# Holding small TensorE steps for a partner, and a placing model with measured durations, in a hybrid S5 and DeltaNet layer

## The chip, the cores and the metric

The kernel runs on one core of a Trainium2 chip. The metric is the device time of one execution in microseconds. Before the change it is 2961.34 us, the median of three runs (2958.78 to 2963.57).

## What is computed

One residual layer on x of 1024 frames by 2048 channels, in float32:

```python
h = rmsnorm(x, ln_w)
proj = h @ w_in                     # 2048 x 10256: u, z_s, q, k, v, z_d, beta, a, gate_s, gate_d
y_s = s5_mixer(u, z_s, ...) @ w_up_s        # 64 groups, 64 complex states each, scan over time, GELU, GLU
y_d = deltanet_mixer(q, k, v, z_d, ...) @ w_up_d   # 8 heads x 128, short conv, chunked delta rule
mixed = sigmoid(gate_s) * y_s + sigmoid(gate_d) * y_d
out = rmsnorm(x + mixed @ w_out, final_norm_w)
```

The delta rule needs, for each head and chunk, the inverse of a unit lower triangular matrix, and then a recurrence over the chunks; S5 needs small projections into and out of its states and a scan over time.

## The kernel before

**Passes and blocks.** The sequence is cut in two passes of T = 512 frames. A pass is a written-out list of blocks. First come ba, then for each head h the blocks k, q, v, z, gd, gd and, shifted by a head or two, u (S5's input). Then come zs (8 blocks, with the last u between them), ud (16), gs (16), glu (8), us (16) and the output projection in four groups of 512 columns. Each block is a product of 128 output channels by 512 frames over 16 k tiles of 128 (8 in ud, glu and us). A k tile takes three f32r matmuls of 128x128 by 512: weights and activations are split in a high and a low part, and hi*hi, hi*lo and lo*hi are added. These are the large products. Weights arrive by DMA in `raw`; `w_prep` copies the high part on ScalarE (`whi`) and subtracts it on VectorE (`wlo`), one chunk of four k tiles at a time. `w_next` keeps LA = 4 chunks split ahead. In the profile's rows X, Y, G0a and G0b are blocks of SBUF that hold the split activations or S5's and the setup's data, and M is the block with DeltaNet's data.

**Lanes.** All other work is written as Python generators, one for each task, queued in lanes: epi (evictions of a block), io (single DMAs), chain (the recurrence of a head, `d_chain`), prep (a head's decay, products and inverse, `d_prep`), tab (S5's tables), s5 (S5's setup `s5_setup`, then `s5_gen` for each of 8 groups of channels), out, and x (`x_gen`, which loads, scales and transposes the next pass's input during the output projection). After each k tile (in the output projection, after each three matmuls) `pump()` goes once over the lanes, and `step(lane)` resumes the first generator of a lane up to its next yield. What the step issues lands at that place in the instruction stream of each engine. The engines run their streams in order, so a step on TensorE that comes before its operands are there holds up every large product behind it.

**The placing model.** While the program is built, `Timed` wraps each engine and books a duration for each instruction in `Clock`, with the data it waits for. A lane's step is taken if its operands are ready on the model's TensorE clock (`job[2] > clk["PE"]` returns) and if the model's VectorE clock is not ahead of TensorE's by more than the lane's slack: 1 us for s5 and tab, 3 for prep, out and x, 4 for chain, SETUP = 2 for the setup. `yield -1` makes the next step ready at once. A head's prep or chain is late when the block number `now` passes its head by more than LATE = 1.0 or 1.4; its slack is then 8, and s5 and tab stand still.

**Drains.** At some places a lane is emptied at once whatever the clocks say (`drain`): epi and io after each block, prep and chain of head i-2 before head i goes on, everything of DeltaNet before ud, s5 before glu, x at the end of the output projection. `d_chain` drains the setup before it writes its first output (`drain("s5", -1)` after its four last transposes), since the setup's scratch lies in that block.

**A head's small products.** `d_prep` has ten steps on TensorE: transposes of k (T), two steps pA (128x128 by 256), transposes of v, then six steps of the inverse, four in 32x32 pieces and two in 64x64. Between pA and the inverse stand 30 small products on GpSimd and a round trip through DRAM (`lu_d`, `tu_d`). `d_chain` has 13 steps on TensorE: three for each of four chunks and a last one with transposes; it starts from `chain_after`, which polls with a bare `yield` until the head's prep is through. `until` polls with `yield -1` until q or v of the head is there. S5 has two steps for each of two halves of a group: the projection into the states (64x128 by 256) and out of them (mostly 128x64 by 256).

Of the kernel before, what the change touches and what calls it, by code (L numbers as in the profile page):

```python
# [18 lines left out]
WAIT = 0.2  # L19
SETUP = 2.0  # L20
LATE = (1.0, 1.4)
MAGIC = float(1.5 * 2 ** 23)
MAGICB = float(1.5 * 2 ** 23 + 127)
LOG2E = float(np.float32(math.log2(math.e)))
# [19 lines left out]
class Clock:  # L44
# [6 lines left out]
    def __init__(self):  # L51
        self.t = {"PE": 0.0, "V": 0.0, "S": 0.0, "G": 0.0, "Q": 0.0, "D": 0.0}
        self.wr, self.rd, self.last = {}, {}, 0.0
        self.slot = {}
        self.table = None

    def cells(self, a):
        name = a.tensor.name
        name = self.slot.get(name) or name.rsplit("_", 2)[0]
        if a.space == bass.MemoryType.DRAM:  # L60
            n = 1 + sum((c - 1) * abs(st) for st, c in a.ap)
            lo, hi = a.offset // 65536, (a.offset + n - 1) // 65536
            return [(name, i) for i in range(lo, hi + 1)]
        ps = a.ap[0][0]
        q = a.offset // ps
        lo = a.offset % ps
        hi = lo + sum((c - 1) * abs(st) for st, c in a.ap[1:])
        parts = range(q // 32, (q + a.ap[0][1] - 1) // 32 + 1)
        return [(name, h, i) for h in parts for i in range(lo // self.CELL, hi // self.CELL + 1)]
# [24 lines left out]
class Timed:  # L94
    def __init__(self, eng, key, clock):
        self.eng, self.key, self.clock = eng, key, clock

    def __getattr__(self, name):
        f = getattr(self.eng, name)
        if name not in COST:  # L100
            return f

        def g(*a, **k):
            o = a[0]
            ck = self.clock
            n = o.free_size()
            ins = [v for v in a[1:] if isinstance(v, bass.AP)]
            ins += [v for kk, v in k.items() if isinstance(v, bass.AP) and kk != "accum_out"]
            outs = [o]
            if self.key == "PE":  # L110
                if name == "transpose":
                    c = 0.11
                elif k["rhs"].dtype == F32R:
                    c = n / 2400
                else:
                    rows = k["lhsT"].shape[0]
                    c = max(n / 600, 0.06) * (0.3 if o.shape[0] <= 32 else 0.5 if min(o.shape[0], rows) <= 64 else 1.0)
                lat = 0.1
            elif name == "dma_start":
                c, lat = 4.0 * n * o.shape[0], 0  # L120
            else:
                fix, per = COST[name][self.key]
                c, lat = fix + per * n, 0.16
                if k.get("op") == ALU.pow:
                    c = 0.25 + 0.17 * n
                if name == "activation":
                    if "accum_out" in k:
                        c += 0.09
                        outs.append(k["accum_out"])
                    fn = a[2] if len(a) > 2 else k["func"]  # L130
                    if fn in TABLES and TABLES[fn] != ck.table:
                        ck.table = TABLES[fn]
                        c += 1.28
            ck.run(self.key, c, outs, ins, lat, name == "dma_start")
            return f(*a, **k)  # L135
        return g


TABLES = {AF.Tanh: 0, AF.Exp: 0, AF.Sin: 1, AF.Ln: 2}
_VG = {"V": (0.07, 1.04e-3), "G": (0.14, 2.1e-3), "S": (0.05, 0.9e-3)}  # L140
_VF = {"V": (0.1, 0.6e-3), "G": (0.12, 1.1e-3), "S": (0.05, 0.9e-3)}
COST = {"tensor_tensor": _VG, "scalar_tensor_tensor": _VG, "tensor_scalar": _VF, "tensor_copy": _VF,
        "tensor_reduce": _VG, "activation": _VG, "tensor_tensor_scan": {"V": (0.07, 1.28e-3)},
        "memset": _VF, "reciprocal": {"V": (0.07, 8.3e-3)}, "iota": _VG, "matmul": None, "transpose": {"V": (0.07, 1.04e-3)}, "dma_start": None}


@with_exitstack
def kernel(
# [25 lines left out]
    clock = Clock()  # L174
    clk = clock.t
    V = Timed(nc.vector, "V", clock)
    S = Timed(nc.scalar, "S", clock)
    G = Timed(nc.gpsimd, "G", clock)
    PE = Timed(nc.tensor, "PE", clock)
# [33 lines left out]
    def tt(o, a, b, op, eng=None):  # L213
        (eng or V).tensor_tensor(o, a, b, op=op)

    def ts(o, a, s1, s2, op0, op1=None):
        if op1 is None:
            V.tensor_scalar(o, a, s1, None, op0=op0)
        else:
            V.tensor_scalar(o, a, s1, s2, op0=op0, op1=op1)  # L220

    def stt(o, a, s, b, op0, op1):
        V.scalar_tensor_tensor(o, a, s, b, op0=op0, op1=op1)
# [76 lines left out]
    def exp_parts(xin, n, scr):  # L300

        c, k, r, q, s = (scr[:, i * n:(i + 1) * n] for i in range(5))
        ts(c, xin, -170.0, 127.0, MAX, MIN)
        ts(k, c, LOG2E, MAGIC, MUL, ADD)
        ts(k, k, MAGIC, None, SUB)
        stt(r, k, -LN2_HI, c, MUL, ADD)
        stt(r, k, -LN2_LO, r, MUL, ADD)
        ts(q, r, 1.0 / 5040, None, MUL)
        for d in (720, 120, 24, 6, 2, 1):
            stt(q, q, 1.0 / d, r, ADD, MUL)  # L310
        ts(c, k, 0.5, MAGIC, MUL, ADD)
        ts(c, c, MAGIC, None, SUB)
        tt(k, k, c, SUB)
# [134 lines left out]
    lanes = {"epi": [], "io": [], "chain": [], "prep": [], "tab": [], "s5": [], "out": [], "x": []}  # L448
    slack = {"epi": 99.0, "io": 99.0, "chain": 4.0, "prep": 3.0, "s5": 1.0, "tab": 1.0, "out": 3.0, "x": 3.0}
# [3 lines left out]
    def late(lane, h):  # L453
        return h >= 0 and now[0] > h + {"prep": LATE[0], "chain": LATE[1]}[lane]

    def late_any():
        return any(lanes[n] and late(n, lanes[n][0][0]) for n in ("prep", "chain"))

    def step(lane):
        q = lanes[lane]  # L460
        while q:
            job = q[0]
            lag = slack[lane] if job[0] >= 0 else SETUP
            if lane in ("chain", "prep") and late(lane, job[0]):
                lag = 8.0
            elif lane in ("s5", "tab") and job[0] >= 0 and late_any():
                return
            if job[2] > clk["PE"] or clk["V"] - clk["PE"] > lag:
                return
            clock.last = 0.0  # L470
            try:
                wait = next(job[1]) or 0.0
            except StopIteration:
                q.pop(0)
                continue
            job[2] = 0.0 if wait < 0 else max(clock.last, wait) + WAIT
            return

    def pump():
        for lane in lanes:  # L480
            step(lane)

    def add(lane, key, gen, at=None):
        lanes[lane].append([key, gen, max(clk["V"], clk["S"]) if at is None else at])
# [117 lines left out]
    def s5_setup(ga, gb, yb):  # L602
# [31 lines left out]
        def vv():  # L634
            a = yb[:, k0[0]:k0[0] + N]
            k0[0] += N
            return a
# [9 lines left out]
        kk, r, hh, ah, s1, c1 = vv(), vv(), vv(), vv(), vv(), vv()  # L647
        ts(kk, th_, INV2PI, MAGIC, MUL, ADD)
        ts(kk, kk, MAGIC, None, SUB)
        stt(r, kk, -PI_C1, th_, MUL, ADD)  # L650
# [735 lines left out]
    for ps_ in range(NPASS):  # L1386
# [49 lines left out]
        for kind, i, c0 in plan[ps_]:  # L1436
# [74 lines left out]
            for k4 in range(nkt // 4):  # L1511
                hi, lo = w_next()
                if kind == "ba":
                    h3 = hi.rearrange("p (k c) -> p k c", k=4)
                    for kl in range(4):
                        kt = k4 * 4 + kl
                        mh, ml = mov(kind, kt)
                        PE.matmul(pb[0:32, :], lhsT=h3[:, kl, 0:32], rhs=mh, start=(kt == 0), stop=False)
                        PE.matmul(pb[0:32, :], lhsT=h3[:, kl, 0:32], rhs=ml, start=False, stop=(kt == nkt - 1))
                        pump()  # L1520
                    continue
                for kl in range(4):
                    kt = k4 * 4 + kl
                    mh, ml = mov(kind, kt)
                    wh, wl = hi[:, kl * P:(kl + 1) * P], lo[:, kl * P:(kl + 1) * P]
                    PE.matmul(pb, lhsT=wh, rhs=mh, start=(kt == 0), stop=False)
                    PE.matmul(pb, lhsT=wh, rhs=ml, start=False, stop=False)
                    PE.matmul(pb, lhsT=wl, rhs=mh, start=False, stop=(kt == nkt - 1))
                    pump()
# [87 lines left out]
        for g in range(4):  # L1617
            pbs = [bank((mainb[0] % 2, 3, 4, 1 - mainb[0] % 2)[t]) for t in range(4)]

            def mm(kt, t, hi, lo):  # L1620
                a, b = (z[:, t * P:(t + 1) * P] for z in kt_of(mh_, kt))
                PE.matmul(pbs[t], lhsT=a, rhs=hi, start=(kt == 0), stop=False)
                PE.matmul(pbs[t], lhsT=a, rhs=lo, start=False, stop=False)
                PE.matmul(pbs[t], lhsT=b, rhs=hi, start=False, stop=(kt == KT - 1))
                pump()
# [68 lines left out]
```

## Time and profile before

| | |
|---|---|
| median of three runs | 2961.34 us |
| profiled execution: time, span | 2961.29 us, 2959.6 us |
| TensorE matmul busy | 2908.3 us, 98% |
| VectorE, ScalarE, GpSimd busy | 1681.5, 1151.8, 410.2 us |
| granted TensorE clock | 0.996 |
| moved by DMA | 409.52 MB, 138 GB/s |

The profile names engines PE (TensorE), PEld (its weight loads), DVE (VectorE), ACT (ScalarE), POOL (GpSimd) and SP. A row of a group gives line, engine, operation, the tile written and the tiles read, then a count, busy time, mean ns of one, and the idle time of the engine ahead of it with what ended that. All instructions go through the wrapper, so all have line 135. A row of the timeline gives start and duration; its x is the count of like instructions that it merges. Matmuls overlap: one of 512 columns shows as 0.39 us long while the next starts after 0.226. A stage's row gives its bounds and length, the busy time and count of PE, PEld, DVE, ACT and POOL, the granted clock, the DMA share and GB/s.

### The profile page before, as it was taken

Reading aid. Unit: us, or ns where it says so; the run is one execution under the profiler, and the core shown is the slowest. Engines: PE = TensorE matmul, PEld = TensorE weight load, DVE = VectorE, ACT = ScalarE, POOL = GpSimd, SP = SyncE. Lnnn points to the kernel's source line nnn. Section 1 sums busy time; section 2 is a strip of 40 time slices with the busy share of each in tenths; the row PEclk is TensorE's granted clock in tenths of the full one; section 3 lists DMA queues with packets and bytes.
Section 4 is the critical chain, followed back from the end, with each engine's and each line's share of the span. In section 5 each row is a group of like instructions: output and inputs, shape, how many; then the busy total and the mean of one; then the engine's idle time right before and its main releaser. Section 6 shows DMA issues by size and latency. Waiting matters only on the chain.

```text
span 2959.6 us, 42410 instructions
## 1 busy us (share of the span) xinstructions
PE 2908.3 (98%) x15840; PEld 2335.3 (79%) x15840; DVE 1681.5 (57%) x3194; ACT 1151.8 (39%) x2487; POOL 410.2 (14%) x792
## 2 busy tenths in 40 slices
PE   8998999999999999999999999999999999999998
PEld 6876777777777788888877777777777788888887
DVE  5746777776767722563444775667656632236542
ACT  5434555554454322334333344333433322223331
POOL 4420222122200000000024211222022000000000
PEclk9999999999999999999999999999999999999999
DMA  6525455445445554446355444544444654445641
GB/s 172 131 74 149 122 132 143 121 123 148 120 128 172 169 149 117 148 136 231 132 164 138 121 122 126 143 124 127 122 139 119 177 171 121 124 123 152 207 138 57
DMA packets 620641, 409.52 MB, mean 138 GB/s; under 512 B 91546, under 2 KB 551571, under 8 KB 618515
## 3 DMA queue, kind: packets, MB, share of 16 engines
q1 hardware_dynamic: 618130, 398.42, 47.1%
q0 software_dynamic: 2304, 8.39, 0.8%
q8 instruction: 125, 2.05, 0.3%
q14 instruction: 82, 0.66, 0.1%
HBM read 339.98 MB, written 66.75 MB: 137 GB/s over the span
## 4 chain that ended last, share of the span: by engine, by line
PE 85%; DVE 5%; POOL 4%; DMA 3%; issue 2%; ACT 2%; SPq 1%; DVEq 0%; POOLq 0%; ACTq 0%
PE p L135 85%; POOL M L135 3%; DVE M L135 1%; DVE G0a L135 1%; DVE wlo L135 1%; DVE Y L135 1%; DMA M<-tu_d 1%; SPq L135 1%; DMA lu_d<-M 1%; ACT M L135 1%; POOL ex L135 1%; DVE tmp L135 0%; DMA M<-lu_d 0%; ACT whi L135 0%; DMA tu_d<-M 0%
## 5 line engine op out<-in xcount | busy, mean ns | idle before, releaser
L135 PE MATMUL p<-X,whi 128*128 128x512 f32 (+1 forms) x4432 | 1395.4, 397 | 2.4 <-DVE whi L135 0.8
L135 DVE TENSOR_TENSOR wlo<-raw,whi 128x512 fp32r<-128x512 f32 x920 | 630.9, 700 | 685.0 <-ACT whi L135 684.0
L135 PEld LDWEIGHTS p<-X,whi 128*128 128x128 f32 (+1 forms) x4432 | 804.7, 187 | 177.3 <-issue 17.5
L135 PE MATMUL p<-X,wlo 128*128 128x512 f32 (+1 forms) x2184 | 852.8, 390 | 10.9 <-DVE wlo L135 10.8
L135 ACT ACTIVATE whi<-raw 128x512 fp32r<-128x512 f32 x917 | 556.0, 625 | 512.2 <-PE p L135 452.9
L135 PE MATMUL p<-Y,whi 128*128 128x512 f32 (+1 forms) x1808 | 568.8, 396 | 0.9 <-ACT p L135 0.9
L135 PEld LDWEIGHTS p<-X,wlo 128*128 128x128 f32 x2184 | 411.0, 188 | 99.9 <-DVE wlo L135 12.0
L135 PEld LDWEIGHTS p<-Y,whi 128*128 128x128 f32 (+1 forms) x1808 | 330.3, 187 | 72.8 <-issue 5.6
L135 PE MATMUL p<-Y,wlo 128*128 128x512 f32 x896 | 349.9, 391 | 2.1 <-DVE wlo L135 2.1
L135 ACT ACTIVATE tmp<-p 128x512 f32<-128x512 f32 x160 | 95.6, 598 | 404.6 <-PE p L135 381.9
L135 POOL TENSOR_TENSOR M<-M 32x28 f32<-32x28 f32 (+8 forms) x492 | 198.9, 404 | 273.7 <-DMA M<-lu_d 185.9
L135 POOL TENSOR_SCALAR smalls<-smalls 128x4 f32<-128x4 f32 (+1 forms) x58 | 15.1, 261 | 1574.7 <-DVE smalls L135 1076.1
L135 DVE TENSOR_TENSOR G0a<-G0a 128x256 f32<-128x256 f32 (+1 forms) x432 | 210.6, 524 | 7.5 <-ACT G0a L135 4.2
L135 PEld LDWEIGHTS p<-Y,wlo 128*128 128x128 f32 x896 | 168.1, 188 | 38.9 <-DVE wlo L135 3.0
L135 PEld LDWEIGHTS p<-M 32*32 32x32 f32 (+2 forms) x3072 | 123.1, 122 | 74.9 <-ACT M L135 27.9
L135 PE MATMUL p<-M 32*32 32x32 f32 (+3 forms) x3072 | 157.2, 216 | 9.0 <-DMA M<-tu_d 3.9
L135 ACT ACTIVATE M<-p 32x128 f32<-32x128 f32 (+3 forms) x323 | 89.9, 281 | 113.8 <-PE p L135 110.4
L135 DVE SCALAR_TENSOR_TENSOR tmp<-tmp,vec 128x512 f32<-128x512 f32 x144 | 108.0, 750 | 9.2 <-ACT tmp L135 5.8
L135 DVE TENSOR_TENSOR G0a<-p,G0a 128x512 f32<-128x512 f32 x128 | 82.0, 682 | 29.2 <-PE p L135 29.2
L135 DVE TENSOR_TENSOR_SCAN G0a<-rho,scar,G0a 128x256 f32<-128x256 f32 x128 | 89.1, 736 | 0.0
L135 PE MATMUL p<-whi,G0a 128*128 128x512 f32 x280 | 88.5, 391 | 0.0
L135 ACT ACTIVATE M<-M 128x128 f32<-128x128 f32 (+2 forms) x98 | 40.2, 412 | 119.5 <-DVE M L135 106.7
(207 smaller groups left out, 2624.6 us busy)
## 6 DMA issues: line engine op xcount, KB each, us to landing
raw<-in_w_in_dram SPq DMA_DIRECT2D x324, 512.0 KB, 4.0
raw<-in_w_out_dram SPq DMA_DIRECT2D x56, 512.0 KB, 4.1
raw<-in_dn_w_up_dram SPq DMA_DIRECT2D x32, 512.0 KB, 4.0
raw<-in_s_w_up_dram SPq DMA_DIRECT2D x32, 512.0 KB, 3.8
td_d<-tmp SPq DMA_DIRECT2D x32, 256.0 KB, 2.3
M<-tu_d SPq DMA_DIRECT2D x32, 256.0 KB, 3.2
cs_d<-G0a SPq DMA_DIRECT2D x32, 256.0 KB, 3.7
yg_d<-G0a SPq DMA_DIRECT2D x64, 128.0 KB, 3.0
```

The source lines that it names most:

```text
L135: return f(*a, **k)
```

## The change

Two things. The placing model gets other durations, and a step that begins on TensorE is held for a while.

Durations (us; n is the number of elements in a partition):

```diff
                 elif k["rhs"].dtype == F32R:
-                    c = n / 2400
+                    c = n / 2400 + 0.0137
+                    if self.apart:
+                        c += 0.09
+                        self.apart = False
                 else:
-                    rows = k["lhsT"].shape[0]
-                    c = max(n / 600, 0.06) * (0.3 if o.shape[0] <= 32 else 0.5 if min(o.shape[0], rows) <= 64 else 1.0)
+                    part = min(o.shape[0], k["lhsT"].shape[0])
+                    c = 0.05 if part <= 32 else max(n / 960, 0.15) if part <= 64 else max(n / 600, 0.2)
+                    if part <= 64 and not self.apart:
+                        c += 0.1
+                    self.apart = True
...
-                        c += 0.09
+                        c += 0.19
...
-_VG = {"V": (0.07, 1.04e-3), "G": (0.14, 2.1e-3), "S": (0.05, 0.9e-3)}
-_VF = {"V": (0.1, 0.6e-3), "G": (0.12, 1.1e-3), "S": (0.05, 0.9e-3)}
+_VG = {"V": (0.17, 1.04e-3), "G": (0.33, 1.95e-3), "S": (0.2, 0.82e-3)}
+_VF = {"V": (0.17, 0.6e-3), "G": (0.22, 1.3e-3), "S": (0.2, 0.82e-3)}
```

`apart` is set by any small f32 product and cleared by the next large one. The pairs are a fixed part and a part for each element. The scan goes from (0.07, 1.28e-3) to (0.1, 2.5e-3), VectorE's transpose from 0.07 to 0.17 fixed. A small f32 matmul of the program shows as two instructions in the profile (a transpose as one).

Holding:

```diff
+HOLD = 6
...
+    on_pe, turns = {}, [0]
+
+    def place(gen):
+        while gen.gi_yieldfrom is not None:
+            gen = gen.gi_yieldfrom
+        return gen.gi_code, gen.gi_frame.f_lineno if gen.gi_frame else 0
...
     def step(lane):
...
+            at = place(job[1])
+            clock.last, clock.products = 0.0, 0
...
+            on_pe[at] = on_pe.get(at, False) or clock.products > 0
...
     def pump():
+        wait = []
         for lane in lanes:
-            step(lane)
+            job = ready(lane)
+            if job is not None:
+                if on_pe.get(place(job[1])):
+                    wait.append(lane)
+                else:
+                    step(lane)
+        if wait:
+            turns[0] += 1
+            if len(wait) > 1 or turns[0] >= HOLD or late_any():
+                turns[0] = 0
+                for lane in wait:
+                    step(lane)
```

`ready` holds the conditions that `step` had. `place` is the line at which a generator stands, and `on_pe` remembers the places from which a resume has issued a TensorE product at least once. A lane at such a place waits until a second lane does so too, until six pumps have counted, or while a head's prep or chain is late. Everything the step issues is held with it, products, evictions and DMAs. `drain` is as before.

More of the change, by code (lines that the diff above doesn't have):

```diff
@@ L55, in __init__ @@
         self.table = None
+        self.products = 0
     def cells(self, a):
@@ L110, in g @@
             if self.key == "PE":
+                ck.products += 1
                 if name == "transpose":
@@ L113, in g @@
                 elif k["rhs"].dtype == F32R:
-                    c = n / 2400
-                else:
-                    rows = k["lhsT"].shape[0]
-                    c = max(n / 600, 0.06) * (0.3 if o.shape[0] <= 32 else 0.5 if min(o.shape[0], rows) <= 64 else 1.0)
+                    c = n / 2400 + 0.0137
+                    if self.apart:
+                        c += 0.09
+                        self.apart = False
+                else:
+                    part = min(o.shape[0], k["lhsT"].shape[0])
[3 more added lines that the diff above has]
+                    self.apart = True
                 lat = 0.1
@@ L139 @@
 TABLES = {AF.Tanh: 0, AF.Exp: 0, AF.Sin: 1, AF.Ln: 2}
-_VG = {"V": (0.07, 1.04e-3), "G": (0.14, 2.1e-3), "S": (0.05, 0.9e-3)}
-_VF = {"V": (0.1, 0.6e-3), "G": (0.12, 1.1e-3), "S": (0.05, 0.9e-3)}
+_VG = {"V": (0.17, 1.04e-3), "G": (0.33, 1.95e-3), "S": (0.2, 0.82e-3)}
+_VF = {"V": (0.17, 0.6e-3), "G": (0.22, 1.3e-3), "S": (0.2, 0.82e-3)}
 COST = {"tensor_tensor": _VG, "scalar_tensor_tensor": _VG, "tensor_scalar": _VF, "tensor_copy": _VF,
-        "tensor_reduce": _VG, "activation": _VG, "tensor_tensor_scan": {"V": (0.07, 1.28e-3)},
-        "memset": _VF, "reciprocal": {"V": (0.07, 8.3e-3)}, "iota": _VG, "matmul": None, "transpose": {"V": (0.07, 1.04e-3)}, "dma_start": None}
+        "tensor_reduce": _VG, "activation": _VG, "tensor_tensor_scan": {"V": (0.1, 2.5e-3)},
+        "memset": _VF, "reciprocal": {"V": (0.07, 8.3e-3)}, "iota": _VG, "matmul": None, "transpose": {"V": (0.17, 1.04e-3)}, "dma_start": None}
 @with_exitstack
@@ L457, in late_any, with ready @@
         return any(lanes[n] and late(n, lanes[n][0][0]) for n in ("prep", "chain"))
-    def step(lane):
[L460 to L466, printed above, removed]
+    def ready(lane):
+        q = lanes[lane]
+        if not q:
+            return None
+        job = q[0]
+        lag = slack[lane] if job[0] >= 0 else SETUP
+        if lane in ("chain", "prep") and late(lane, job[0]):
+            lag = 8.0
+        elif lane in ("s5", "tab") and job[0] >= 0 and late_any():
+            return None
+        if job[2] > clk["PE"] or clk["V"] - clk["PE"] > lag:
+            return None
+        return job
+    on_pe, turns = {}, [0]
[3 more added lines that the diff above has]
+        return gen.gi_code, gen.gi_frame.f_lineno if gen.gi_frame else 0
+    def step(lane):
+        while True:
+            job = ready(lane)
+            if job is None:
                 return
-            if job[2] > clk["PE"] or clk["V"] - clk["PE"] > lag:
-                return
-            clock.last = 0.0
+            at = place(job[1])
+            clock.last, clock.products = 0.0, 0
             try:
@@ L473, in step @@
             except StopIteration:
-                q.pop(0)
+                lanes[lane].pop(0)
                 continue
+            on_pe[at] = on_pe.get(at, False) or clock.products > 0
             job[2] = 0.0 if wait < 0 else max(clock.last, wait) + WAIT
@@ L479, in pump @@
     def pump():
+        wait = []
         for lane in lanes:
-            step(lane)
+            job = ready(lane)
+            if job is not None:
[9 more added lines that the diff above has]
+                    step(lane)
     def add(lane, key, gen, at=None):
```

## The prediction

> **What bounds the kernel now.** I read the head of the page, then busy time by stage, then the list of who waited for whom on TensorE in the two stages that hold small products, then single stretches of the timeline.
>
> ```profile
> span 2959.6 us, 42410 instructions
> PE 2908.3 (98%) x15840; PEld 2335.3 (79%) x15840; DVE 1681.5 (57%) x3194; ACT 1151.8 (39%) x2487; POOL 410.2 (14%) x792
> PE 85%; DVE 5%; POOL 4%; DMA 3%; issue 2%; ACT 2%; SPq 1%; DVEq 0%; POOLq 0%; ACTq 0%
> ```
>
> TensorE is the bound, and 85% of the chain that ended last is its own work. The table by stage (length, then busy time and instructions of each engine) shows where anything is left:
>
> ```profile
> 218.00:230.00 12.00, 1.38 (x6) 0.88 (x5) 11.69 (x12) 1.11 (x2) 0.00 (x0) 0.72 0.07 25
> 230.00:933.00 703.00, 694.54 (x4263) 549.38 (x4263) 507.17 (x1054) 359.97 (x788) 120.98 (x260) 1.00 0.50 135
> 1028.00:1333.00 305.00, 305.00 (x1347) 252.56 (x1346) 125.28 (x191) 90.33 (x158) 2.16 (x5) 1.00 0.49 144
> 1515.00:2385.00 870.00, 860.95 (x5169) 676.67 (x5170) 549.93 (x1057) 332.64 (x815) 197.98 (x363) 1.00 0.50 137
> ```
>
> From 1028 to 1333 the large products run alone, one per 305.00 / 1347 = 0.226 us; no order makes that shorter. What an order can win lies in the DeltaNet and S5 stages: up to 230, 230 to 933, 1515 to 2385. The waits of TensorE there, first 100 to 1030, then 1515 to 2390 (total us, times, longest):
>
> ```profile
> PE p L135 <- DVE wlo L135: 10.6, 1, 10.6
> PE p L135 <- DMA M<-tu_d: 2.6, 2, 1.5
> PE p L135 <- DMA G0b<-v_d: 2.5, 2, 1.6
> PE p L135 <- ACT G0b L135: 1.1, 1, 1.1
> PE p L135 <- DVE M L135: 1.1, 3, 0.7
> ...
> PE p L135 <- issue: 2.5, 2, 1.4
> PE p L135 <- DVE wlo L135: 2.1, 1, 2.1
> PE p L135 <- DMA M<-tu_d: 1.3, 3, 0.5
> ```
>
> So the prize is small: one wait of 10.6 us, and some 13 us in a dozen short ones. The rest of the loss is the small products themselves and the change from large to small and back.
>
> **The change part by part.** *Durations of the placing model.* Against the rows of the trace:
>
> ```profile
> L135 DVE TENSOR_TENSOR wlo<-raw,whi 128x512 fp32r<-128x512 f32 x920 | 630.9, 700 | 685.0 <-ACT whi L135 684.0
> L135 ACT ACTIVATE whi<-raw 128x512 fp32r<-128x512 f32 x917 | 556.0, 625 | 512.2 <-PE p L135 452.9
> L135 POOL TENSOR_TENSOR M<-M 32x28 f32<-32x28 f32 (+8 forms) x492 | 198.9, 404 | 273.7 <-DMA M<-lu_d 185.9
> ```
>
> The VectorE product over 512 elements goes from 0.07 + 0.53 = 0.60 to 0.70 us (row: 0.700), the ScalarE copy from 0.51 to 0.62 (0.625), the GpSimd product of 28 elements from 0.20 to 0.38 (0.404), a large matmul from 0.213 to 0.227 (0.226). A k tile (three products) advances the model by 0.68 instead of 0.64 us, 6%, while VectorE and ScalarE ops grow by 17 to 21% at 512 elements and far more at small sizes. A lane step that waits for other engines will thus come some k tiles later: the 30 GpSimd products of the inverse of each head count 30 x 0.19 = 5.7 us more. No instruction is added for this; a step that comes later costs TensorE nothing as long as large products fill the gap, and in these stages they do.
>
> What it takes away is steps placed before their operands. I charge the waits for tu_d (2.6 + 1.3; these steps come after the GpSimd inverse, which the old model undercounts most), v_d and G0b (2.5 + 1.1), and VectorE's M (1.1): 8.6 us, of which I take 8. A wait shows as idle only after the modelled end of the matmul before (0.39 us, as in the rows below, where the issue is 0.226), so each of these 11 hides another 0.16: 2 us. The wait of 2.1 for wlo is an overrun of VectorE, which the new costs brake sooner: half, 1 us. The 2.5 of "issue" stay. Together 11 us; the ends are 0 (other steps wait instead) and 13 (8.6 + 2.1 and 2 hidden).
>
> *The long wait.* On VectorE and then TensorE:
>
> ```profile
> 203.83 2.43 PE L135 MATMUL p<-Y,G0a 128*32 128x32 f32 x32
> 207.69 0.60 PE L135 MATMUL p<-ident,M 128*128 128x128 f32 x4
> 209.37 4.29 DVE L135 SCALAR_TENSOR_TENSOR G0b<-ident,G0b 128x128 f32<-128x128 f32 x16
> 213.57 14.73 DVE L135 TENSOR_TENSOR Y<-Y 128x1024 f32<-128x1024 f32 x12
> 229.61 0.80 PE L135 MATMUL p<-X,wlo 128*128 128x512 f32 x1 [10.62 <-DVE wlo L135]
> ```
>
> Four transposes at 207.69 are the last product step of head 0's chain; behind them d_chain drains the S5 setup, so that 4.29 + 14.73 = 19 us of VectorE stand ahead of the next weight chunk. Four chunks are split ahead, 16 k tiles of 0.68 = 10.9 us; the rest is the wait. The change does not touch the drain. It would go only if the setup had finished, that is if the chain's last step came 19 us later against the setup. Both lanes get dearer on VectorE, the setup with its many small operations more; a w0 group like that at 203.83 was charged 8 x 0.03 + 8 x 0.018 = 0.4 us and is now 1.8, which lets the chain go ahead, not fall behind. And holding is off there: after block z of head 1 head 0's chain is late (now = 1.43 > 1.4), and late_any() opens the gate. I take no change (0), with ends of +4 (the chain so far ahead that another 4.29 us of such work is left to the drain) and -12 (the whole stretch 218 to 230).
>
> *Holding.* A held step issues nothing new; it goes up to 5 pumps later, 5 x 0.68 = 3.4 us. What pairing saves is seen in groups between large products (TensorE; start, busy):
>
> ```profile
> 330.03 0.61 PE L135 MATMUL p<-X,whi 128*128 128x512 f32 x2
> 330.48 0.39 PE L135 MATMUL p<-X,wlo 128*128 128x512 f32 x1
> 330.80 0.44 PE L135 MATMUL p<-M 32*32 32x32 f32 x16
> 331.17 0.73 PE L135 MATMUL p<-X,whi 128*128 128x512 f32 x2
> 331.74 0.39 PE L135 MATMUL p<-X,wlo 128*128 128x512 f32 x1
> ...
> 332.75 0.45 PE L135 MATMUL p<-M 32*32 32x32 f32 x32
> ...
> 620.06 0.44 PE L135 MATMUL p<-M 32*32 32x32 f32 x16
> 620.43 1.13 PE L135 MATMUL p<-G0b 64*128 64x256 f32 x8
> 621.49 0.74 PE L135 MATMUL p<-X,whi 128*128 128x512 f32 x2
> ```
>
> Before a group in part of the array the step is 0.32 (330.48 to 330.80) instead of 0.226, and the two large products behind it take 0.57 (331.17 to 331.74) instead of 0.45: 0.09 + 0.12 = 0.21 us per group. At 620 two such groups stand together; the second starts 0.37 after the first, its bare time, so the pair pays that once. Groups over the whole array differ:
>
> ```profile
> 2282.98 0.39 PE L135 MATMUL p<-X,wlo 128*128 128x512 f32 x1
> 2283.20 0.60 PE L135 MATMUL p<-state,M 128*128 128x128 f32 x4
> ...
> 2284.11 0.40 PE L135 MATMUL p<-X,wlo 128*128 128x512 f32 x1
> ...
> 2288.27 0.40 PE L135 MATMUL p<-Y,wlo 128*128 128x512 f32 x1
> 2288.50 0.39 PE L135 MATMUL p<-M 128*128 128x128 f32 x2
> ...
> 2289.20 0.40 PE L135 MATMUL p<-Y,wlo 128*128 128x512 f32 x1
> ```
>
> Four cost 1.13 - 0.68 = 0.45, two 0.93 - 0.68 = 0.25: 0.10 each and some 0.05 for the group. So pairing pays 0.2 us only where both groups use part of the array: six of a head's ten prep steps and the 64 steps of S5. The chain's 13 steps a head and the transposes give 0.05.
>
> How often does it pair? A lane whose next resume can begin on TensorE counts as waiting even when it only polls. chain_after's yield runs into the chain's first products, so it is marked once for all; the same holds for the yield in until. Through head h's inverse its chain sits in chain_after: prep is never held there, and S5 meets it only by chance. Holding bites on the chain while prep is empty, on prep's transposes and pA, on S5 alone. I take one pair of partial groups a head beyond today's (16 x 0.2 = 3 us) less 1 us for the chain's pairs, unseen: -2 us, with ends of 0 and 64 x 0.21 = -13.
>
> The Trainium skill, "TensorEngine Tiling (Array Packing)", section "Key Properties", says that changing the tiling mode, not just the tile, drains TensorE. The 0.21 us of the partial groups agrees; by the rule alone a mixed pair would also save one change of mode, for which the rows above show nothing.
>
> *What waits behind a held step.* The lane's own later steps, its evictions on ScalarE and VectorE, its DMAs on SP: all are written only with the step, so no queue blocks. The chain of a head grows by at most 13 x 3.4 = 44 us; a head lasts at least 7 x 16 k tiles x 0.68 = 76 us, the chain is drained two heads on, and its late rule lifts the hold before. S5 of pass 0 is done when the dense stage begins at 1028, and is needed after the 16 gs blocks, 16 x 16 x 0.68 = 174 us later. I take nothing for either. The x lane is tight:
>
> ```profile
> L135 PE MATMUL p<-ident,tmp x64: 270/272/273, 1395.1 to 1455.7; 128*128 128x128 f32 x64
> L135 SPq DMA_DIRECT2D tmp<-in_final_norm_w_dram x4: 422/430/573, 1508.1 to 1509.7; - x4
> ```
>
> It runs alone, so all five resumes of each quarter at a place with products are held: 4 x 5 x 3.4 = 68 us, from 1456 to 1524, past the stage's end, where the second row's loads follow drain("x"). Two transposes would be left to it; their operands are there, and the next pass needs them 14 k tiles in. +1 us, ends 0 and +7 (a load landing inside the drain). New short waits elsewhere: +1.
>
> Sum: 2961.3 (profiled execution; the median is the same to 0.05) - 11 + 0 - 2 + 1 + 1 = 2950 us.
>
> **The rivals.** *The setup finishes before the drain* (for: 19 us is a few steps; against: the w0 charge above): a further 12, 2938. *Every pairing pays 0.21 us*, whole-array groups included: chain and prep have 16 x 23 steps and S5 has 64, 432 in all; with 100 pairs among them 21 us instead of 2, 2931. For it, the partial groups; against it, the 0.05 of the whole-array ones. (This is what the Trainium skill's rule under "Key Properties" of "TensorEngine Tiling (Array Packing)" comes to when every step counts as a change of mode; the rows so far bear it out for the partial groups alone.) *The waits move*: the old ones go, as many new ones come, 2961; for it, they are rare and scattered already. *VectorE overruns TensorE*, the slower one: the new model overcharges TensorE: 32 instructions of 32x32 count 16 x 0.05 + 0.19 = 0.99 where 16 count 0.59, although the rows show them busy 0.45 and 0.44, and a whole-array group gets 0.09 where the rows show 0.05. Per head that is 2 x 0.4 and 17 x 0.04 (13 chain and 4 prep groups) and, for the group of 64, 0.9 by the same slope: 2.4 us by which VectorE seems less behind than it is. With the chain's slack of 4 and a step of 3 its true lag passes 3 chunks, 8.2 us, and TensorE waits for wlo, by 2.1 us (the one such wait above) in each of 16 heads: 2950 + 34 = 2984. It decides once the true lag passes 8.2 us; against it, VectorE is busy 507.17 of 703.00 us, and its new costs brake it.
>
> **How the numbers follow.** My forecast (2944 to 2957) 0.45, setup finishes 0.15, every pairing 0.06, waits move 0.20, overrun 0.14. A measurement here tells 0.2%, 5.9 us, from no change. Faster: 0.15 + 0.06 and most of 0.45, 0.58; same 0.27; slower 0.15. The range runs from 2935, between the two fast rivals, to 2968, short of the overrun.
>
> **What would show it.** Right: waits for tu_d, v_d and G0b near zero; 1028 to 1333 as dense as now; the wait of about 10 us for wlo near 218 still there; the chain's steps further apart; the last p<-ident,tmp past 1500. Wrong: that long wait gone or doubled, fresh waits for wlo in the heads, or a wait of TensorE at 1515.

## The result, and the profile after

The changed kernel takes 3010.61 us (median of four runs, 3009.8 to 3011.11), the kernel before 2961.74 us on the same chip: a ratio of 1.0161 [1.0149, 1.0173]. The prediction was 2950 us, faster, with a range from 2935 to 2968. The profiled execution took 3011.01 us.

The head of the page after, with the rows of TensorE's busy share and granted clock in 40 slices of 75 us:

```profile
span 3009.3 us, 42332 instructions
PE 2912.6 (97%) x15840; PEld 2346.9 (78%) x15840; DVE 1682.0 (56%) x3194; ACT 1146.8 (38%) x2487; POOL 384.7 (13%) x792
...
PE   7998999999999998599999999999999999999998
...
PEclk9999999999999999699999999999999999999999
```

The work is the same. One slice, the 17th, is half empty and has a clock of 0.6. That is the end of the gs blocks and the start of glu in pass 0. By stage (bounds and length, then busy time and instructions of PE, PEld, DVE, ACT and POOL, the clock, DMA share, GB/s):

```profile
230.00:909.00 679.00, 667.52 (x4129) 536.17 (x4128) 433.83 (x853) 320.47 (x727) 115.92 (x265) 0.99 0.48 129
1001.00:1173.00 172.00, 172.00 (x778) 138.81 (x777) 88.99 (x179) 66.61 (x108) 0.00 (x0) 1.00 0.47 135
1173.00:1263.00 90.00, 38.17 (x125) 22.47 (x124) 50.61 (x112) 19.89 (x34) 4.54 (x8) 0.62 0.31 100
1573.00:2430.00 857.00, 852.34 (x5148) 678.68 (x5148) 544.33 (x1051) 329.10 (x811) 175.24 (x355) 0.99 0.50 135
```

The two DeltaNet stages are shorter, 679 us where it was 703 and 857 where it was 870, but they do not hold the same work: the first row counts 4129 products on TensorE where it was 4263, since S5's come later and some large ones fall outside it, and the last 5148 where it was 5169. Between them, 1173 to 1263 holds 38.17 us of TensorE work in 90. The waits of TensorE from 1150 to 1262 (total us, times, longest) and, below, the same stretch in order of time:

```profile
PE p L145 <- DVE G0a L145: 25.6, 6, 7.1
PE p L145 <- DMA G0a<-yg_d: 14.3, 2, 14.1
PE p L145 <- issue: 8.6, 1, 8.6
PE p L145 <- ACT G0b L145: 2.7, 2, 1.4
PE p L145 <- DMA G0b<-yg_d: 0.6, 2, 0.3
```

```profile
1184.05 0.39 PE L145 MATMUL p<-X,wlo 128*128 128x512 f32 x1
...
1191.77 1.97 PE L145 MATMUL p<-G0a,G0b 128*64 128x256 f32 x6 [6.32 <-DVE G0a L145]
...
1195.10 2.08 PE L145 MATMUL p<-G0b 64*128 64x256 f32 x8 [1.36 <-ACT G0b L145]
...
1205.73 1.19 PE L145 MATMUL p<-G0b,G0a 128*128 128x256 f32 x2 [8.55 <-issue]
...
1218.24 1.97 PE L145 MATMUL p<-G0a,G0b 128*64 128x256 f32 x6 [7.14 <-DVE G0a L145]
...
1235.02 1.97 PE L145 MATMUL p<-G0a,G0b 128*64 128x256 f32 x6 [4.58 <-DVE G0a L145]
...
1251.09 1.22 PE L145 MATMUL p<-G0a,whi 128*128 128x512 f32 x2 [14.10 <-DMA G0a<-yg_d]
```

This is `drain("s5")` ahead of glu. S5 is not through: its last halves of groups run here one after the other, most products waiting for VectorE's rotations and scans (for the 8.6 us of "issue" the profile names no releaser), with no large product to fill the gaps, and at the end glu waits 14.1 us for its own input to come back through DRAM. The waits add up to 51.8 us. The rest of the loss is S5's bare products and the clock, 0.62 on average, which is why 38 us are busy for so little work.

From the starts of the blocks in both traces: gs block 15, the last ahead of glu, begins at 1191.1 before and at 1173.4 after, so the changed kernel is then 17.7 us ahead. From there to the end of the first glu block it takes 88.7 us where 16.4 were needed, 72.3 lost. From there to the end it gains 4.9. The sum, -17.7 + 72.3 - 4.9 = 49.7, is the difference of the two profiled executions (3011.01 - 2961.29). Taken at face value, the change without the drain would stand at -22.6 us, near 2938. That is too much: a part of the 17.7 us is S5's products, which are only put off into the drain. In the run with S5 free (below), where all of them are done by then, gs block 15 begins at 1178.4, 12.7 us ahead.

How late S5 is shows in its out-projection: first and last start of p<-G0a,G0b from 700 to 1262, before and after.

```profile
L135 PE MATMUL p<-G0a,G0b x64: 377/379/431, 720.3 to 1014.6; 128*64 128x256 f32 x64
```

```profile
L145 PE MATMUL p<-G0a,G0b x96: 377/379/688, 716.3 to 1236.4; 128*64 128x256 f32 x96
```

The last product moved from 1014.6 to 1236.4, past the place where it is needed. In the last large stretch it had 174 us to spare; something took all of it.

### The profile page after: what moved, and what is told of

It is laid out like the page before. It is cut to its first block, busy times and chain, and to the rows that moved or that the text cites. A ratio compares the mean times of both kernels' runs of the same rounds, so it can differ in the third digit from the quotient of the medians.

```text
span 3009.3 us, 42332 instructions
## 1 busy us (share of the span) xinstructions
PE 2912.6 (97%) x15840; PEld 2346.9 (78%) x15840; DVE 1682.0 (56%) x3194; ACT 1146.8 (38%) x2487; POOL 384.7 (13%) x792
## 4 chain that ended last, share of the span: by engine, by line
PE 93%; DVE 2%; DMA 1%; ACT 1%; POOL 1%; issue 0%; SPq 0%; DVEq 0%; POOLq 0%; ACTq 0%
PE p L145 93%; DVE G0a L145 1%; POOL ex L145 1%; DVE Y L145 1%; DVE M L145 0%; DMA M<-in_x_dram 0%; DMA G0b<-yg_d 0%; DMA M<-tu_d 0%; POOL M L145 0%; SPq L145 0%; ACT G0b L145 0%; ACT L145 0%; ACT G0a L145 0%; DMA yg_d<-G0a 0%; DVE wlo L145 0%
## 5 line engine op out<-in xcount | busy, mean ns | idle before, releaser
L145 POOL TENSOR_TENSOR M<-M 32x28 f32<-32x28 f32 (+8 forms) x492 | 178.1, 362 | 165.3 <-DMA M<-lu_d 73.4
L145 POOL TENSOR_TENSOR M<-M,causal 128x512 f32<-128x512 f32 x16 | 20.6, 1290 | 526.1 <-ACT M L145 458.2
```

## The experiments

**The two halves of the change.** First the durations alone, with the old pump:

```diff
     def pump():
-        wait = []
         for lane in lanes:
-            job = ready(lane)
-            ...
+            step(lane)
```

> The new durations alone; pump steps each lane at once, as before. Theory A (the whole loss is S5's lane of pass 0: held and blocked, it is not through when glu begins, and the drain there costs 72 us; everything else became faster by 17.7 + 5 = 23 us): the lane is through in time, no drain at the end of gs, and the time is about 2961 - 23 = 2938 us if the gain comes from the durations. Rival B (the durations themselves slow S5, since the dearer VectorE keeps its lane, with 1 us of slack, from stepping): the drain stays, 2990 to 3010 us. Rival C (the gain came from holding): 2955 to 2965 us.

Then the holding alone, with the old durations (all lines of the model as before, `HOLD` and the new `pump` kept):

> The holding alone, with the old durations. Theory A with the gain from the durations: S5 slower than before but through before glu, since the old VectorE costs let it step sooner; the short waits of before partly stay; 2950 to 2961 us. Rival C (the gain came from holding): about 2938 us. Rival D (holding alone makes S5 too late): the drain of before glu is there, 2990 us or more.

Measured: durations alone 2955.44 us, ratio 0.9977 [0.9967, 0.9986]; holding alone 2962.18 us, 1.000 [0.9991, 1.001]. Neither has the drain: from the start of gs block 15 to the end of the first glu block both take 16.3 us. Each half is harmless, and the two together lose 1.6%. Neither half brings the gain either: of the values expected, 2955 is that of rival C and not the 2938 of theory A, and holding alone gains nothing, which rules out rival C in turn. S5's last product in the two:

```profile
L145 PE MATMUL p<-G0a,G0b x80: 377/379/431, 709.8 to 1116.3; 128*64 128x256 f32 x80
```

```profile
L139 PE MATMUL p<-G0a,G0b x72: 377/379/431, 708.9 to 1093.7; 128*64 128x256 f32 x72
```

1116.3 with the durations, +102 us; 1093.7 with holding, +79 us. Added to 1014.6 that is 1196 (an estimate: the two delays need not simply add). glu begins at 1202.0 in the kernel before, and in the changed one, 17.7 us ahead, it would begin near 1184, with GELU, GLU's input and its way through DRAM still to come after the last product. Either alone fits in the slack; the two do not.

**S5 never held.**

```diff
-                if on_pe.get(place(job[1])):
+                if lane != "s5" and on_pe.get(place(job[1])):
```

> The change, but S5's lane is never held; all other lanes are, and durations are the new ones. Theory A: no drain at the end of gs, 2938 us (2930 to 2945). Rival E (S5 is late because chain and prep, held, become late and late_any() stops the s5 and tab lanes, not because S5 itself is held): the drain stays in part, 2970 to 3000 us.

Measured: 2946.64 us, 0.9948 [0.9933, 0.9963]. TensorE has no wait left between 1150 and 1262, and S5's last product starts at 1150.1. So taking away that one lane's holding is enough to undo the loss, and the rest of the change then gains 0.5%. The time is just above the 2930 to 2945 us that theory A gave.

**S5 and the tables do not stand still while a head is late.** The other thing that delays them:

```diff
-        elif lane in ("s5", "tab") and job[0] >= 0 and late_any():
+        elif lane in ("s5", "tab") and job[0] >= 0 and late_any() and False:
```

> The change, but s5 and tab no longer stand still while a head's prep or chain is late; S5's lane is held as in the change. Theory A with rival E as its cause: S5 is through before glu, 2938 us (2930 to 2950). If S5's own holding is the cause: the drain stays, 2985 to 3010 us.

Measured: 2954.09 us, 0.997 [0.996, 0.998], S5's last product at 1172.1. This lies between the two expectations. It too cures the drain, but only just: from gs block 15 to the end of the first glu block it takes 27.1 us instead of 16.3, glu comes before its data, and the row of the waits over the whole run is

```profile
PE p L145 <- DMA G0a<-yg_d: 5.1, 4, 2.6
```

Three things thus draw on the same slack: the dearer VectorE costs against S5's lag of 1 us, the stops for late heads, and S5's own holding. Taking away either of the last two is enough, and so is going back to the old durations (holding alone, above).

**Chain and prep not held.** If holding delayed the heads, made them late and so stopped S5, freeing the heads would cure it; if it is S5's own holding, it would not.

```diff
-                if on_pe.get(place(job[1])):
+                if lane not in ("chain", "prep") and on_pe.get(place(job[1])):
```

> The change, but chain and prep are never held; S5 and x are. With free S5 (the run before) the drain ahead of glu went. Theory F (S5's own holding and the dearer VectorE are enough; what chain and prep do is secondary): the drain stays, 60 to 75 us of it, 2995 to 3015 us. Rival E (S5 is late because held chain and prep run late and late_any() stops it): the drain goes, 2938 to 2950 us.

Measured: 3011.42 us, 1.0156 [1.0142, 1.0169], and S5's last product at 1234.2. The waits of TensorE from 1150 to 1262 are those of the changed kernel:

```profile
PE p L145 <- DVE G0a L145: 25.6, 6, 7.2
PE p L145 <- DMA G0a<-yg_d: 14.4, 2, 14.1
```

So theory F holds: S5's own holding and the new durations are enough, freeing the heads changes nothing, and freeing S5 (above) removes the drain. The heads are not without effect, though. How often S5 is passed by can be counted in the kernels themselves while the program is built, pump by pump up to glu of pass 0. A pump stands under the first cause that applies, in the order of the columns; pumps at which S5 only waits for operands are left out.

| kernel | a head is late | VectorE's lag | held | S5 is stepped |
|---|---|---|---|---|
| before | 15 | 438 | 0 | 298 |
| durations alone | 80 | 577 | 0 | 298 |
| holding alone | 108 | 421 | 93 | 298 |
| the change | 216 | 523 | 101 | 248 |
| the change, chain and prep not held | 81 | 573 | 211 | 248 |

The durations add stops of both of the first two kinds, holding adds late heads and holds of S5 itself, and with both S5 is 50 steps short at glu. Where the heads are not held, fewer of them are late, but S5 is then held itself instead: the one delay takes the place of the other.

Why S5 is held for so long can be read in the code: `on_pe` marks a place as soon as one resume from it begins on TensorE. `yield -1 if h == 0 else 0` and the `yield -1` behind the copy of pY are each one line for two cases, only one of which begins with a product. A group of S5 is held at seven resumes, of which four begin on TensorE. In the late blocks no other lane is there to release it, so each costs up to 3.4 us: 8 x 7 x 3.4 = 190 us at most, of which 79 were seen with holding alone.

**S5 and x never held.**

```diff
+                if lane not in ("s5", "x") and on_pe.get(place(job[1])):
```

> The change, but neither S5 nor x is held. Against the run with S5 free alone (2946.6 us), x's transposes end near 1445 instead of 1502, and the wait of 3.2 us between the last of them and the next product goes: 2943 us (2940 to 2945). If x's holding costs nothing, 2946 to 2947.

Measured: 2944.44 us, 0.993 [0.9918, 0.9942]. In the kernel with only S5 free, the start of pass 1 (1480 to 1512) still showed the first row below; with x free too (1400 to 1512) it is the other two:

```profile
PE p L145 <- DVE M L145: 2.9, 1, 2.9
```

```profile
PE p L145 <- DVE M L145: 1.6, 1, 1.6
PE p L145 <- ACT p L145: 0.9, 1, 0.9
```

The 1.6 us stand at 1411, in the output projection, where S5 free alone has 0.9 us of the same wait. At the start of pass 1 the wait goes from 2.9 to 0.9 us, most of what was expected. The two ratios differ by 0.0018, some 5 us, with intervals that overlap. The traces settle it. I counted the large products of each trace (those that read whi or wlo) and took the time from one in the output projection (number 5000, at 1361.6 us before) to one early in pass 1 (number 5700, at 1529.1). Against the kernel before, the four with x held and the new durations take 4.4 to 5.9 us longer (the changed kernel 4.4, S5 free 5.9); all eight with the new durations in which x is not held take 1.8 longer. So holding x costs 2.6 to 4.1 us.

**A shorter hold, and the setup's tail on GpSimd.** With S5 and x free, `HOLD` from 6 to 3; and the same with the last 12 products of the setup (128x1024, the 14.73 us of VectorE ahead of the long wait) on GpSimd:

```diff
-            tt(v1, re, bc(ar, 32), MUL)
+            tt(v1, re, bc(ar, 32), MUL, eng=G)
...
```

> S5 and x free and HOLD 3 instead of 6, so a held step of chain or prep goes up to 2 pumps later, not 5. If the gain over the durations alone (2955 us) comes from pairing, fewer pairs form and the time lies between, 2945 to 2950 us; if it comes from the operands having more time, 2 pumps are enough, 2940 to 2944 us.

> As the next kernel (S5 and x free, HOLD 3), and the last twelve products of S5's setup (128x1024) run on GpSimd instead of VectorE. Theory: the wait of 9 to 11 us for wlo at 220 to 250 is the 14.7 us that they hold VectorE in the drain; it goes, and the clock stays granted: 10 to 12 us below the next kernel, about 2933 us. Rival: GpSimd takes over 2 us for each, head 1's inverse waits behind 25 us of it and the next drain of chain and prep takes the gain back: no difference, or slower by up to 10 us.

Measured: hold of 3, 2936.08 us, 0.9906 [0.9891, 0.9921], the fastest of all, ahead of both kernels and below both expectations, nearer to the one in which the operands have more time. With the tail on GpSimd 2946.66 us, 0.9938 [0.9925, 0.995], 10.6 us slower, about what its rival gave, but by another way, as the rows show. VectorE's timeline with the tail on VectorE, and then VectorE, GpSimd and TensorE with it on GpSimd:

```profile
226.49 2.69 DVE L145 SCALAR_TENSOR_TENSOR G0b<-ident,G0b 128x128 f32<-128x128 f32 x8
229.11 14.57 DVE L145 TENSOR_TENSOR Y<-Y 128x1024 f32<-128x1024 f32 x12
```

```profile
227.08 16.99 DVE L145 SCALAR_TENSOR_TENSOR G0b<-ident,G0b 128x128 f32<-128x128 f32 x8
```

```profile
227.48 26.82 POOL L145 TENSOR_TENSOR Y<-Y 128x1024 f32<-128x1024 f32 x12
```

```profile
247.47 1.12 PE L145 MATMUL p<-ident,M 128*128 128x128 f32 x4 [15.09 <-DVE M L145]
```

VectorE was given less to do and took as long: eight products went from 2.69 to 16.99 us. The long wait did not go, it became 15.09 us, for VectorE's M.

**Is it pairs, or time?** With S5 and x free, a hold of 2; and a hold of 2 where a partner releases nothing, so that each step of chain and prep comes exactly one pump later and never because another lane is there:

```diff
+                if lane not in ("s5", "x") and on_pe.get(place(job[1])):
+                    own[lane] = own.get(lane, 0) + 1
+                    if own[lane] < HOLD and not late_any():
+                        continue
+                    own[lane] = 0
+                step(lane)
```

> S5 and x free, HOLD 2: a step of chain or prep that begins on TensorE goes at most one pump later. Theory G (what holding brings is time for the operands, and one k tile of 0.68 us covers most short waits): 2934 to 2942 us, about as HOLD 3 (2936). Theory H (it brings pairs): fewer pairs than with HOLD 3, nearer to the durations alone, 2943 to 2955 us.

> S5 and x free; each such step of chain and prep goes exactly one pump later by a count of its own lane, and a partner releases nothing, so pairs form by chance alone. Theory G: as HOLD 2, 2932 to 2942 us. Theory H: the gain over the durations alone goes, 2950 to 2957 us.

And no holding at all: the old pump, the new durations, and a step of chain and prep counted as ready 0.5 us after its operands instead of 0.2:

```diff
-            job[2] = 0.0 if wait < 0 else max(clock.last, wait) + WAIT
+            job[2] = 0.0 if wait < 0 else max(clock.last, wait) + (0.5 if lane in ("chain", "prep") else WAIT)
```

> The new durations and the old pump, no holding; every step of chain and prep that waits for operands waits 0.5 us behind them instead of 0.2. Theory G: most of the gain comes without any holding, 2935 to 2947 us, with the short waits of TensorE for ACT G0b (S5, not delayed here) left. Theory H: as the durations alone, 2952 to 2958 us.

Measured: hold of 2, 2946.66 us, 0.9939 [0.9926, 0.9953]; without partners 2940.74 us, 0.9919 [0.9907, 0.9931]; no holding but 0.3 us more margin 2939.48 us, 0.9915 [0.9901, 0.9928], level with the hold of 3. The last two came out as theory G said. The hold of 2 did not: it lies in the range of theory H. But theory H cannot be the reason, since leaving the partner out made it 5.9 us faster, not slower; a little time for the operands is what gains. Among the holds of 6, 3 and 2 (0.993, 0.9906, 0.9939) the order is not that of their length. For the hold of 2 the groups of the table below show where it lies: counted in the same way it has 434 groups with some 14 us of waits in them, against 7.2 at a hold of 3 and 5.4 without a partner. A reading that fits, not tested further: a partner sends a step at once, and with so short a hold that often leaves its operands no time. The hold of 6 has some 8 us of such waits, so why it stays behind the hold of 3 is open; a part of it is seen in the table as less waiting between large products at 3.

The traces say the same. I took every group of small products between two large ones after 100 us, its cost as the time from the large product before it to the second behind it, less two large products. What groups of the same composition cost at their cheapest (the lowest fifth over all the kernels) is the bare cost, the rest a wait; a composition that is rare has little but itself to be measured against. The last column but one is the change of all three sums against before.

| kernel | groups | bare cost, us | waits in groups | extra between large products | change of the sum | change of the profiled time |
|---|---|---|---|---|---|---|
| before | 452 | 317.7 | 31.2 | 16.4 | | |
| durations alone | 445 | 318.0 | 19.0 | 22.4 | -5.9 | -5.4 |
| holding alone | 400 | 320.2 | 25.6 | 19.5 | 0.0 | +0.7 |
| S5 free | 426 | 318.8 | 10.5 | 20.7 | -15.3 | -14.4 |
| S5, x free, hold 3 | 428 | 318.0 | 7.2 | 14.5 | -25.6 | -25.3 |
| no partner, hold 2 | 438 | 319.0 | 5.4 | 20.2 | -20.7 | -19.7 |
| later, no hold | 442 | 318.0 | 4.2 | 21.5 | -21.6 | -21.8 |

The sums close to within a microsecond. The bare cost is nearly the same with 452 groups as with 400: fewer and larger groups save nothing that this count can see. The gain is waits that go, and most of those do not show in the list of waits at all: a group that starts some tenths late is hidden under the modelled end of the product before it.

**One chunk more ahead of the drain.** With the hold of 3, one more `w_prep` at d_chain's drain of the setup:

```diff
+            if ps_ == 0 and wst["prep"] <= wst["use"] + LA - 1:
+                w_prep()
```

> S5 and x free, HOLD 3, and ahead of the drain of S5's setup one more weight chunk is split (five buffers are there, four are in use). One chunk is 4 k tiles of 0.68 us: the wait for wlo near 235 falls from 8.7 to about 6 us and the time by 2.7, to 2933 us (2931 to 2936). If the wait ends with something other than VectorE's backlog, 2936 stays.

Measured: 2937.57 us, 0.9907 [0.9893, 0.992], the same as without, and the long wait still there (waits of TensorE, 100 to 1262):

```profile
PE p L145 <- DVE wlo L145: 8.7, 1, 8.7
PE p L145 <- DVE M L145: 1.3, 1, 1.3
```

In this kernel the setup is emptied by the drain in the block u 0, ahead of d_chain's, so the extra chunk was written behind the VectorE work that it should have preceded. The expectation missed that. What a deeper lookahead at the right place would bring stays open.

## Why the prediction was wrong, point by point

**The step that failed** was to cost S5's lateness at nothing. It is in "What waits behind a held step": "S5 of pass 0 is done when the dense stage begins at 1028, and is needed after the 16 gs blocks, 16 x 16 x 0.68 = 174 us later. I take nothing for either." The deadline and the slack were right. What was not done is the sum against it. For the x lane the prediction did multiply: four quarters, five held resumes, 3.4 us each. For S5 the same working gives up to 8 x 7 x 3.4 = 190 us, more than 174; holding alone took 79 of it. And the first part, on the durations, had charged nothing for a step that comes later "as long as large products fill the gap", without asking how late S5 would be by the sum of its steps: +102 us by the runs. The two parts were each costed at nothing, one by one, against a slack they share, and together they used it up: 72.3 us lost in the drain. The prediction also counted on the late rule to take the hold off the chain, and left out that by the same rule S5 stands still meanwhile, at 216 pumps instead of 15; without that stop the kernel takes 2954.09 us. A rival with that mechanism, S5 past its drain, was missing, although the list of drains names "s5 before glu". It would have been the one on the other side, instead of the overrun.

**Short waits go: -11.** Right in kind, too small. Waits of TensorE from 230 to 1150 after:

```profile
PE p L145 <- DVE wlo L145: 11.0, 1, 11.0
PE p L145 <- ACT G0b L145: 0.4, 1, 0.4
```

Those for tu_d, v_d and M are gone there, and in the second stage tu_d has 0.3 us left of 1.3 (rows below). With S5 free the waits in groups fall by 20.7 us, 4.3 of it given back between large products. The prediction took 0.16 us hidden in each of the 11 waits that the list shows; the table says that many groups waited without a row in that list.

**The long wait: 0.** Right: 10.6 before, 11.0 after, and the rows below show the same drain on VectorE, 2.69 + 15.19 us, eight instead of sixteen of the small products.

```profile
227.16 2.69 DVE L145 SCALAR_TENSOR_TENSOR G0b<-ident,G0b 128x128 f32<-128x128 f32 x8 [8.44 <-ACT G0b L145]
229.78 15.19 DVE L145 TENSOR_TENSOR Y<-Y 128x1024 f32<-128x1024 f32 x12
```

The rival in which the setup is through before the drain did not come about.

**Pairing: -2.** Not seen, with the sign unproved: the bare cost of all groups did not fall (+0.3 to +2.5 us). The rows at 620 did show a pair that paid the entry once; over a whole run such pairs are too few to see, and the rival that made every pairing pay falls. So does, for the total, the reading of the Trainium skill's rule in "TensorEngine Tiling (Array Packing)", "Key Properties", by which every group counts as a change of mode: with holding alone there are 52 fewer groups, and their bare cost and waits together fall by only 3.1 us, 0.06 for each, where that rival has 0.21.

**The x lane: +1.** Right in place, short in size. The transposes and what followed the last of them:

```profile
L145 PE MATMUL p<-ident,tmp x64: 270/272/273, 1457.3 to 1570.0; 128*128 128x128 f32 x64
...
1569.69 0.60 PE L145 MATMUL p<-ident,tmp 128*128 128x128 f32 x4
...
1573.20 3.00 PE L145 MATMUL p<-Y,whi 128*32 128x512 f32 x7 [2.91 <-DVE M L145]
```

The last one starts 3.5 us ahead of pass 1, in the drain, as foreseen, and a wait of 2.9 us stands behind it. With x free (and S5) 0.9 us are left there, as before the change. By the count of large products above, holding x costs 2.6 us in the changed kernel instead of 1, inside the ends of 0 and +7.

**The overrun of VectorE: did not come.** The waits for wlo in the heads after, 1573 to 2440, are one of 3.1 us beside the 2.1 before.

```profile
PE p L145 <- DVE wlo L145: 3.1, 1, 3.1
PE p L145 <- DVE M L145: 2.9, 1, 2.9
PE p L145 <- DMA state<-st_d: 1.0, 1, 1.0
PE p L145 <- DMA M<-tu_d: 0.3, 1, 0.3
```

With S5 free the kernel takes 0.9948 x 2961.3 = 2946 us, inside the likeliest case's 2944 to 2957. That the rest of the sum comes out so near is in part luck: more waits went than were charged, pairing saved nothing that shows, and x cost more. The missing term was 72 us.

## What to carry to other kernels

When a step is made to wait, multiply the wait by the number of such steps of each lane and hold the product against that lane's deadline, most of all for a lane that runs alone; and add up all parts of the change that draw on the same slack before calling any of them free. A hard drain at a deadline turns lateness into full loss: here a chain that had hidden under large products cost nothing until it was late, and then 72.3 us, part of them at a lower clock. Before crediting a scheduler's idea (here, pairs) with a gain, run it with the idea removed and its side effect kept: 0.3 us more margin, without any holding, gave about as much.

## What the runs showed of the hardware

VectorE and GpSimd got in each other's way far more than I had expected. With 12 products of 128x1024 on GpSimd (26.82 us, 2.24 each), VectorE's 128x128 scalar_tensor_tensor beside them took 16.99 / 8 = 2.12 us each, against 2.69 / 8 = 0.34 without: VectorE got through about one instruction for each of GpSimd's. The Trainium skill, "SBUF — State Buffer", section "Who interferes with whom", says that a VectorE instruction with two SBUF inputs contends with a GpSimd instruction that reads SBUF, and calls the port pair that they share an exclusive lock; the trace agrees.

The clock after a gap: in the 90 us around the drain the granted clock was 0.62 on average, and the first pair of large products behind the wait of 14.10 us shows 1.22 us where 0.61 is usual, so that work between waits is slow as well as late.
